# Block products of a feed-forward layer: weights fetched a group ahead, a matmul divided at another column, feature sums reloaded in wider pieces

## The chip, the cores and the metric

The kernel runs on one core of one Trainium2 chip. The metric is the device time of one execution in microseconds (us), the median over the runs. The engines are called as in the profile: PE (TensorE matmul), PEld (TensorE weight load), DVE (VectorE), ACT (ScalarE), POOL (GpSimd), SP (SyncE, which here only issues DMAs).

## What is computed

A block of a diffusion model on 512 tokens and 2048 features: a token mixer (a state-space branch and a long-convolution branch), then a gated feed-forward layer. The change lies in the feed-forward layer alone:

```python
def swiglu(h, wg, wu, wd):
    return (jax.nn.silu(h @ wg) * (h @ wu)) @ wd

h = modulate(x, norm_ffn_pre[layer], sh2, sc2)
x = x + g2 * rmsnorm(swiglu(h, w_gate[layer], w_up[layer], w_down[layer]), norm_ffn_post[layer])
```

`h` has 512 tokens x 2048 features, the two first weights are 2048 x 5632, the last is 5632 x 2048.

## The kernel before

All work is in fp32, done as three matmuls on a number split in two: `hi` is the value rounded to the fp32r type by ACT (a CAST), `lo` is the rest, by DVE (a TENSOR_TENSOR, subtract). A product is then hi·hi + hi·lo + lo·hi. Tiles of split weights are `whi` and `wlo` (three buffers each), those of split features `fh`/`fl` and `th`/`tl`.

Most of the feed-forward layer is a loop over 54 **quads** (`quad(q)`). A quad is a 2x2 group of weight blocks, each 128x1024, times a 2x2 group of feature blocks, computed with seven block products instead of eight (a Strassen-like scheme). The quads come as gate, up, gate, up, ... for 38 of them, 0 to 37 (even ones of `w_gate`, odd ones of `w_up`), then 16 of `w_down` (`w_ds`), 38 to 53.

Each of the seven products is a `body`, 8 x 3 matmuls of 256 columns, so a quad has 168 matmuls. `body` 0 to 6 use the weights r11, r12, r22, r21, r11 again, r22 again, r12 again. Between them the weights are changed in place: r21 gets the fourth block added and r11 the third block, both by an accumulating DMA that POOL issues (L163, `accum_op=ADD`); then DVE adds r11 into r22 and r22 into r12 (L80, `rq<-rq,rq`). `feed` does for each body: ACT cast to `whi`, DVE subtract to `wlo`, and then gives the matmuls of the body fed two steps before. So a body's weights are split two bodies ahead of their matmuls. A call of `feed` is a **step**, seven to a quad.

After the products DVE forms the four results R of the quad (`early` after body 5, `end` after body 6). In an up quad `end` multiplies with the gate's R, SP stores R to `hd` (L163, `hd<-R`), DVE forms sums T of R that the seven products of `w_down` need (`sums`, three operations), and SP stores T (`hd<-T`). The last pairs, blocks 19 to 21, have no T. In the gate quads a piece of an unrelated vector product is carried along (`ada`: a load `rt<-in_ada` into the buffer that T also uses, then two DVE operations `ada<-rt,cc,ada`).

At quad 38 and again at quad 46 the features are exchanged (`replace`): the products' eight input tiles are loaded from `hd` in 128x256 pieces and split by ACT and DVE (L1368, L1370), six sets of eight pieces spread over the steps, two splits of a set in a step.

Order: the loop's loads and splits stay in program order on their queues (`keep_in_program_order`), SP issues its DMAs one after the other, and a DMA that has to wait (for a buffer, or for the result that it stores) holds all that stand behind it. The other operations on DVE and ACT are placed by a scheduler.

The first matmul of body 0 is divided in two, columns 0 to 159 and 160 to 255, in every third quad (`KICK = 160`, `q % 3 == 0`).

Of the kernel before, what the change touches and what calls it, by code (L numbers as in the profile page):

```python
# [65 lines left out]
def block_kernel(ctx: ExitStack, tc: tile.TileContext, I: dict, out: bass.AP, dbg=None, stop=None):  # L66
    nc = tc.nc
# [11 lines left out]
    def tt(e, o, a, b, op):  # L79
        e.tensor_tensor(out=o, in0=a, in1=b, op=op)  # L80
# [87 lines left out]
    def wraw(ap):  # L168
        raw = wp.tile([128, 1024], F32, tag="raw", bufs=3, name=nm("raw"))
        n = ap.shape[-1]  # L170
        dma(raw[:, :n], ap)
        return raw

    def wload(ap, eng=nc.vector):
        raw = wraw(ap)
        n = ap.shape[-1]
        hi = wp.tile([128, 1024], F32R, tag="whi", bufs=3, name=nm("whi"))
        lo = wp.tile([128, 1024], F32R, tag="wlo", bufs=3, name=nm("wlo"))
        nc.scalar.copy(out=hi[:, :n], in_=raw[:, :n])  # L179
        tt(eng, lo[:, :n], raw[:, :n], hi[:, :n].bitcast(F32), SUB)  # L180
        return [(hi[:, o : min(o + 128, n)], lo[:, o : min(o + 128, n)]) for o in range(0, n, 128)]
# [1140 lines left out]

    CH = ([3 + i for i in range(8)], [11 + i for i in range(8)])
    CP = [0, 1, 2, 19, 20, 21]
    KICK = 160

    def place(j, k, area):
        if j == 0:
# [12 lines left out]
    def at(n, fn):  # L1341
        hooks.setdefault(n, []).append(fn)
# [20 lines left out]
    def op_load(dst, src):  # L1363
        dma(dst[1].bitcast(F32), src)
# [6 lines left out]

    def replace(q, c, area):

        for j in range(1, 7):
            n = 7 * (q - 1) + j
            for k in range(8):
                d = place(j, k, 0)
                at(n + 3, lambda d=d, k=k, j=j: op_load(d, hd[CH[c][k]][:, SRC[j], :]))
                at(n + 5 + k // 2, lambda d=d: op_split(d))
        for k in range(8):  # L1380
            d = place(0, k, area)
            at(7 * (q - 4) + k, lambda d=d, k=k: op_load(d, hd[CH[c][k]][:, 0, :]))
            at(7 * (q - 4) + k + 2, lambda d=d: op_split(d))
# [9 lines left out]
        dma(raw, ap)  # L1393
        return raw

    def load_s1(q):
        r = qload("raw", quads[q][0][1, 0])
        dma(r, quads[q][0][1, 1], nc.gpsimd, accum_op=ADD)
        return r

    y2d = dram.tile([2, 8, 128, 4, 256], F32, name="y2d")
    gate = {}
    pin[0] = True
# [4 lines left out]
        return raw  # L1408

    ada_raw[0] = raw_t  # L1410
    nxt = {"r11": qload("ra", quads[0][0][0, 0]), "r12": qload("ra", quads[0][0][0, 1]), "r21": load_s1(0)}

    def quad(q):
        src, area, kind, m = quads[q]
        ps = {}
        R = gu.tile([128, 4, 256], F32, tag="R", bufs=2, name=nm("R"))

        def body(i):
            def run(w):
                if i in (0, 2, 3, 5):  # L1420
                    ps[i] = acc()
                b, o = {0: (0, 0), 1: (0, 1), 2: (2, 1), 3: (3, 1), 4: (3, 0), 5: (5, 0), 6: (2, 0)}[i]
                p = ps[b][:, o * 256 : o * 256 + 256]
                for k in range(8):
                    xh, xl = place(i, k, area)
                    wh, wl = w[k]

                    for c0, c1 in ((0, KICK), (KICK, 256)) if i == k == 0 and q % 3 == 0 else ((0, 256),):
                        nc.tensor.matmul(p[:, c0:c1], wh, xh[:, c0:c1], start=k == 0 and c0 == 0, stop=False,  # L1429
                                         skip_group_check=True)  # L1430
                    nc.tensor.matmul(p, wh, xl, start=False, stop=False, skip_group_check=True)  # L1431
                    nc.tensor.matmul(p, wl, xh, start=False, stop=k == 7, skip_group_check=True)  # L1432
                if i == 5:
                    late.append(early)
                if i == 6:
                    late.append(end)

            return run

        def early():  # L1440
            p12, p75, p6 = ps[0], ps[3], ps[5]
            nc.scalar.copy(out=R[:, 0, :], in_=p12[:, 0:256])
            tt(nc.vector, R[:, 0, :], p6[:, 0:256], R[:, 0, :], SUB)
            tt(nc.vector, R[:, 2, :], R[:, 0, :], p75[:, 0:256], SUB)
            tt(nc.vector, R[:, 1:4:2, :], R[:, 0:4:2, :], p75[:, 256:512].unsqueeze(1).broadcast_to([128, 2, 256]), ADD)
            nc.scalar.copy(out=R[:, 0, :], in_=p12[:, 0:256])
            tt(nc.vector, R[:, 0, :], R[:, 0, :], p12[:, 256:512], ADD)

        def end():

            tt(nc.vector, R[:, 1:3, :], R[:, 1:3, :], ps[2].rearrange("p (a b) -> p a b", a=2), SUB)
            if kind == "w_gate":
                act(R[:, 0, :], R[:, 0, :], AF.Silu)
                act(R[:, 1, :], R[:, 1, :], AF.Silu, scale=-1.0)
                act(R[:, 2:4, :], R[:, 2:4, :], AF.Silu)
# [12 lines left out]

        def sums(m, R):
            T = gu.tile([128, 4, 256], F32, tag="T", name=nm("T"))  # L1470
            tt(nc.vector, T[:, 0:4:2, :], R[:, 1:4:2, :], R[:, 0:2, :], SUB)
            tt(nc.vector, T[:, 1, :], R[:, 3, :], T[:, 0, :], SUB)
            tt(nc.vector, T[:, 3, :], T[:, 1, :], R[:, 2, :], SUB)
            dma(hd[m][:, 4:8, :], T)


        r11, r12, r21 = nxt["r11"], nxt["r12"], nxt["r21"]
        more = q + 1 < len(quads)
        r22 = qload("raw", src[1, 1])
        feed(r11, body(0))  # L1480
        feed(r12, body(1))
        feed(r22, body(2))
        dma(r11, src[1, 0], nc.gpsimd, accum_op=ADD)
        feed(r21, body(3))
        if more:
            nxt["r11"] = qload("ra", quads[q + 1][0][0, 0])
        feed(r11, body(4))
        if more:
            nxt["r21"] = load_s1(q + 1)
        tt(nc.vector, r22, r22, r11, ADD)  # L1490
        feed(r22, body(5))
        if more:
            nxt["r12"] = qload("ra", quads[q + 1][0][0, 1])
        tt(nc.vector, r12, r12, r22, ADD)
        feed(r12, body(6))
        if kind != "w_up" and q < NG + 4:
            ada(1)

# [16 lines left out]
        quad(q)  # L1515
    while pend:
        pend.pop()()
    first = [wload(I["w_dc"][0])]

    def rest():  # L1520
        for op in late:
# [6 lines left out]
    rest()  # L1528
    w, fn = ahead.pop(0)
    fn(w)  # L1530
    first.append(wload(I["w_dc"][1]))
    rest()
    w, fn = ahead.pop(0)
    fn(w)
# [227 lines left out]
```

## Time and profile before

| | us |
|---|---|
| median of 3 runs | 2620.09 (2610.10 to 2623.55) |
| profiled execution | 2608.34 |
| its span, first to last instruction | 2606.6 |
| quads 0 to 37 (gate, up) | 809.76 |
| quads 38 to 53 (w_down) | 340.1 |
| all 54 quads, of the span | 1149.85 |

Quads 0 to 53 run from 1278.03 to 2427.88 us of the span, and what lies ahead of and behind them is not touched by the change, except for the two first loads behind the last quad. A quad's start is the start of the first matmul of its body 0. PE is busy for 2410.9 of 2606.6 us, but matmuls overlap, so what a quad costs is read from its length, not from the busy time. DVE is busy for 1880.5 us, ACT for 985.4 us.

### The profile page before, as it was taken

The numbers are of one execution on the slowest core, as the hardware profiler recorded it, in microseconds if no ns is written. First come the engines' busy times: TensorE is split into PE (matmuls) and PEld (weight loads), VectorE is DVE, ScalarE is ACT, GpSimd is POOL, SyncE is SP. The second block draws the span as 40 slices with busy tenths as digits, with TensorE's granted clock in tenths as the row PEclk, the third lists the DMA queues.
The fourth block names the chain that finished last, engine by engine and source line by source line (L and its number), as shares of the span: only waits on it lengthen the run. The fifth ranks groups of instructions, "written<-read, shape, count | busy, mean of one in ns | idle before, by whom it ended". The sixth has DMA issues, their size and how long they took to land.

```text
span 2606.6 us, 41025 instructions
## 1 busy us (share of the span) xinstructions
PE 2410.9 (92%) x16102; PEld 2145.6 (82%) x16102; DVE 1880.5 (72%) x2494; ACT 985.4 (38%) x1437; POOL 554.7 (21%) x537
## 2 busy tenths in 40 slices
PE   8999989899999999999998999999989989899895
PEld 3467779577667788989998999899989989899785
DVE  7986756888878776789776767676767776677444
ACT  3143325222123322455434343343434444444233
POOL 1230010665623245740000000000000000000104
PEclk9999999999999999999999999999999999999998
DMA  8867745445356666456857575757576777877843
GB/s 289 319 214 244 228 156 165 146 139 171 114 197 201 242 230 205 149 175 188 236 146 211 160 212 158 209 159 208 157 210 171 209 229 217 227 213 182 261 135 121
DMA packets 183721, 508.71 MB, mean 195 GB/s; under 512 B 19583, under 2 KB 65599, under 8 KB 181992
## 3 DMA queue, kind: packets, MB, share of 16 engines
q1 hardware_dynamic: 166824, 445.27, 50.3%
q0 software_dynamic: 16704, 60.82, 13.2%
q8 instruction: 126, 2.06, 0.3%
q14 instruction: 67, 0.55, 0.1%
HBM read 454.12 MB, written 51.90 MB: 194 GB/s over the span
## 4 chain that ended last, share of the span: by engine, by line
PE 34%; DMA 13%; DVE 5%; issue 3%; ACT 2%; POOL 1%; SPq 0%; POOLq 0%; DVEq 0%; ACTq 0%
DMA rq<-in_w_up 9%; PE acc L1432 9%; PE acc L1431 9%; PE acc L1429 9%; PE acc L83 8%; DVE wlo L80 2%; DMA rq<-in_w_ds 1%; ACT whi L1347 1%; DMA x<-x1d 1%; DMA y<-y2d 1%; DMA rt<-in_ada 0%; DVE R L80 0%; DMA tl<-hd 0%; POOL gs L80 0%; POOL rq L163 0%
## 5 line engine op out<-in xcount | busy, mean ns | idle before, releaser
L1347 ACT CAST whi<-rq 128x1024 fp32r<-128x1024 f32 x378 | 397.3, 1051 | 614.5 <-PE acc L1431 376.2
L80 DVE TENSOR_TENSOR wlo<-rq,whi 128x1024 fp32r<-128x1024 f32 x378 | 459.3, 1222 | 187.6 <-ACT whi L1347 183.2
L1432 PE MATMUL acc<-th,wlo 128*128 128x256 f32 x1728 | 491.7, 285 | 50.6 <-DVE wlo L80 50.6
L1429 PE MATMUL acc<-th,whi 128*128 128x256 f32 x1728 | 489.4, 283 | 10.5 <-ACT whi L1347 10.5
L1431 PE MATMUL acc<-tl,whi 128*128 128x256 f32 x1728 | 488.8, 283 | 0.0
L179 ACT CAST whi<-raw 128x1024 fp32r<-128x1024 f32 (+1 forms) x220 | 225.7, 1026 | 503.5 <-PE acc L83 295.5
L1432 PEld LDWEIGHTS acc<-th,wlo 128*128 128x128 f32 x1728 | 334.6, 194 | 55.3 <-DVE wlo L80 55.2
L1429 PE MATMUL acc<-fh,whi 128*128 128x256 f32 (+2 forms) x1314 | 362.2, 278 | 4.4 <-ACT fh L1368 4.4
L1432 PE MATMUL acc<-fh,wlo 128*128 128x256 f32 x1296 | 361.7, 279 | 2.5 <-DVE wlo L80 2.5
L1431 PE MATMUL acc<-fl,whi 128*128 128x256 f32 x1296 | 362.2, 279 | 0.0
L80 DVE TENSOR_TENSOR wlo<-raw,whi 128x1024 fp32r<-128x1024 f32 x204 | 265.4, 1301 | 121.2 <-ACT whi L179 116.4
L1429 PEld LDWEIGHTS acc<-th,whi 128*128 128x128 f32 x1728 | 334.8, 194 | 11.4 <-ACT whi L1347 11.4
L1431 PEld LDWEIGHTS acc<-tl,whi 128*128 128x128 f32 x1728 | 335.6, 194 | 0.0
L83 PE MATMUL acc<-hh,whi 128*128 128x512 f32 x688 | 285.1, 416 | 3.9 <-ACT hh L74 3.7
L83 PE MATMUL acc<-hl,whi 128*128 128x512 f32 x688 | 277.6, 403 | 3.6 <-DVE hl L77 3.6
L83 PE MATMUL acc<-hh,wlo 128*128 128x512 f32 x688 | 276.9, 402 | 0.0
L1429 PEld LDWEIGHTS acc<-fh,whi 128*128 128x128 f32 x1314 | 247.0, 189 | 4.8 <-ACT fh L1368 4.5
L1432 PEld LDWEIGHTS acc<-fh,wlo 128*128 128x128 f32 x1296 | 244.8, 189 | 3.4 <-DVE wlo L80 3.3
L1431 PEld LDWEIGHTS acc<-fl,whi 128*128 128x128 f32 x1296 | 245.8, 190 | 0.1
L77 DVE SCALAR_TENSOR_TENSOR ada<-raw,cc,ada 128x512 f32<-128x512 f32 x200 | 171.7, 859 | 45.2 <-DMA raw<-in_ada 42.3
L80 DVE TENSOR_TENSOR rq<-rq,rq 128x1024 f32<-128x1024 f32 x108 | 131.9, 1221 | 97.4 <-DMA rq<-in_w_up 85.6
L83 PE MATMUL acc<-fh,wlo 128*128 128x256 f32 (+1 forms) x512 | 160.0, 313 | 14.4 <-DVE wlo L80 14.4
(333 smaller groups left out, 4513.6 us busy)
## 6 DMA issues: line engine op xcount, KB each, us to landing
raw<-in_ada SPq DMA_DIRECT2D x107, 512.0 KB, 4.1
rq<-in_w_gate SPq DMA_DIRECT2D x76, 512.0 KB, 9.6
rq<-in_w_up SPq DMA_DIRECT2D x76, 512.0 KB, 5.8
ada<-in_ada SPq DMA_DIRECT2D x64, 512.0 KB, 4.4
rq<-in_w_ds SPq DMA_DIRECT2D x64, 512.0 KB, 5.7
raw<-in_w_hy SPq DMA_DIRECT2D x44, 512.0 KB, 4.0
raw<-in_w_out SPq DMA_DIRECT2D x41, 512.0 KB, 4.2
raw<-in_w_xbc SPq DMA_DIRECT2D x38, 512.0 KB, 4.0
```

The source lines that it names most:

```text
L77: nc.vector.scalar_tensor_tensor(out=o, in0=a, scalar=s, in1=b, op0=op0, op1=op1)
L80: e.tensor_tensor(out=o, in0=a, in1=b, op=op)
L83: nc.tensor.matmul(o, lhsT, rhs, start=start, stop=stop)
L179: nc.scalar.copy(out=hi[:, :n], in_=raw[:, :n])
L1347: nc.scalar.copy(out=hi, in_=raw)
L1429: nc.tensor.matmul(p[:, c0:c1], wh, xh[:, c0:c1], start=k == 0 and c0 == 0, stop=False, skip_group_check=True)
L1431: nc.tensor.matmul(p, wh, xl, start=False, stop=False, skip_group_check=True)
L1432: nc.tensor.matmul(p, wl, xh, start=False, stop=k == 7, skip_group_check=True)
```

## The change

1. **Weights.** Each quad issues the loads of all four weight blocks of the next quad: r11 ahead of its first `feed`, r12 and r21 after it, r22 after the fifth. Before, r11, r21 and r12 of the next quad were issued after the fourth, fifth and sixth `feed`, and r22 of the quad itself at its start. The accumulating DMA into r11 is issued after the second `feed` (before: the third), and the one into r21 of the next quad right behind it. Buffers are as many as before. Behind the last quad the two first blocks of the next stage come the same way.
2. **Division of a matmul.** At 16 columns (16 and 240) in place of 160 (160 and 96), in every second quad in place of every third, that is in 27 quads in place of 18.
3. **Feature sums.** At quads 38 and 46, four of the six sets are loaded in pairs, 128x512 a piece, and split in pieces of that size, four in a step. The two others stay as they were.

```diff
-    def wload(ap, eng=nc.vector):
-        raw = wraw(ap)
+    def wload(ap, eng=nc.vector, raw=None):
+        raw = wraw(ap) if raw is None else raw
...
-    KICK = 160
+    KICK = 16
...
     def replace(q, c, area):
-        for j in range(1, 7):
-            n = 7 * (q - 1) + j
+        n = 7 * (q - 1)
+        for j, load, first in ((1, 4, 6), (6, 9, 11)):
             for k in range(8):
                 d = place(j, k, 0)
-                at(n + 3, lambda d=d, k=k, j=j: op_load(d, hd[CH[c][k]][:, SRC[j], :]))
-                at(n + 5 + k // 2, lambda d=d: op_split(d))
+                at(n + load, lambda d=d, k=k, j=j: op_load(d, hd[CH[c][k]][:, SRC[j], :]))
+                at(n + first + k // 2, lambda d=d: op_split(d))
+        for o, load, first in ((2, 7, 9), (0, 8, 10)):
+            for k in range(8):
+                d = [t[:, o : o + 2, :] for t in tx[k]]
+                at(n + load, lambda d=d, k=k, o=o: op_load(d, hd[CH[c][k]][:, 4 + o : 6 + o, :]))
+                at(n + first + k // 4, lambda d=d: op_split(d))
...
-                    for c0, c1 in ((0, KICK), (KICK, 256)) if i == k == 0 and q % 3 == 0 else ((0, 256),):
+                    for c0, c1 in ((0, KICK), (KICK, 256)) if i == k == 0 and q % 2 == 0 else ((0, 256),):
...
-        r11, r12, r21 = nxt["r11"], nxt["r12"], nxt["r21"]
+        r11, r12, r21, r22 = nxt
         more = q + 1 < len(quads)
-        r22 = qload("raw", src[1, 1])
+        nsrc = quads[q + 1][0] if more else None
+        n11 = qload("ra", nsrc[0, 0]) if more else None
         feed(r11, body(0))
+        n12 = qload("ra", nsrc[0, 1]) if more else None
+        n21 = qload("raw", nsrc[1, 0] if more else I["w_dc"][0])
         feed(r12, body(1))
+        dma(r11, src[1, 0], nc.gpsimd, accum_op=ADD)
+        if more:
+            dma(n21, nsrc[1, 1], nc.gpsimd, accum_op=ADD)
         feed(r22, body(2))
-        dma(r11, src[1, 0], nc.gpsimd, accum_op=ADD)
         feed(r21, body(3))
-        if more:
-            nxt["r11"] = qload("ra", quads[q + 1][0][0, 0])
         feed(r11, body(4))
-        if more:
-            nxt["r21"] = load_s1(q + 1)
         tt(nc.vector, r22, r22, r11, ADD)
+        n22 = qload("raw", nsrc[1, 1] if more else I["w_dc"][1])
         feed(r22, body(5))
-        if more:
-            nxt["r12"] = qload("ra", quads[q + 1][0][0, 1])
         tt(nc.vector, r12, r12, r22, ADD)
         feed(r12, body(6))
```

Three places show what moves. The first is SP's queue in a gate quad, here quad 4, up to the loads of the up quad behind it; of that up quad, quad 5, rq_11877, 11908, 11941 and 11977 are r11, r21, r12 and r22 before.

```order
L163 DMA hd<-R_11519 128x1024
L163 DMA hd<-T_11818 128x1024
L163 DMA rq_11877<-in_w_up 128x1024
L163 DMA rq_11908<-in_w_up 128x1024
L163 DMA rq_11941<-in_w_up 128x1024
L163 DMA rt_11972<-in_ada 128x1024
L163 DMA rq_11977<-in_w_up 128x1024
```

The same place in the changed kernel, where r11, r12, r21 and r22 of quad 5 are rq_11746, 11777, 11779 and 11915.

```order
L163 DMA rq_11746<-in_w_up 128x1024
L163 DMA rq_11777<-in_w_up 128x1024
L163 DMA rq_11779<-in_w_up 128x1024
L163 DMA hd<-R_11522 128x1024
L163 DMA hd<-T_11826 128x1024
L163 DMA rq_11915<-in_w_up 128x1024
L163 DMA rt_11975<-in_ada 128x1024
```

Three of the four loads of the up quad now stand ahead of the two stores, and `rt` has one load ahead of it instead of three.

The second place is DVE from the end of the gate quad to the subtraction for body 3 of the up quad (the same quad 5). Before:

```order
L80 TENSOR_TENSOR wlo_11980<-rq_11877,whi_11979 128x1024
L80 TENSOR_TENSOR R_11743<-acc_11983,R_11743 128x256
L80 TENSOR_TENSOR R_11743<-R_11743,acc_11916 128x256
L77 SCALAR_TENSOR_TENSOR ada_7630<-rt_11972,cc,ada_7630 128x512
L80 TENSOR_TENSOR R_11743<-R_11743,acc_11916 128x2x256
L77 SCALAR_TENSOR_TENSOR ada_7630<-rt_11972,cc,ada_7630 128x512
L80 TENSOR_TENSOR R_11743<-R_11743,acc_11823 128x256
L80 TENSOR_TENSOR wlo_12009<-rq_11941,whi_12008 128x1024
L80 TENSOR_TENSOR R_11743<-R_11743,acc_11883 128x512
L80 TENSOR_TENSOR wlo_12043<-rq_11977,whi_12042 128x1024
L80 TENSOR_TENSOR rq_11977<-rq_11977,rq_11877 128x1024
L80 TENSOR_TENSOR wlo_12077<-rq_11908,whi_12076 128x1024
```

And in the changed kernel, from `ada` on:

```order
L77 SCALAR_TENSOR_TENSOR ada_7630<-rt_11975,cc,ada_7630 128x512
L80 TENSOR_TENSOR wlo_11983<-rq_11746,whi_11982 128x1024
L77 SCALAR_TENSOR_TENSOR ada_7630<-rt_11975,cc,ada_7630 128x512
L80 TENSOR_TENSOR R_11745<-acc_11986,R_11745 128x256
L80 TENSOR_TENSOR R_11745<-R_11745,acc_11921 128x256
L80 TENSOR_TENSOR wlo_12016<-rq_11777,whi_12015 128x1024
L80 TENSOR_TENSOR R_11745<-R_11745,acc_11921 128x2x256
L80 TENSOR_TENSOR R_11745<-R_11745,acc_11889 128x512
L80 TENSOR_TENSOR wlo_12052<-rq_11915,whi_12051 128x1024
L80 TENSOR_TENSOR R_11745<-R_11745,acc_11831 128x256
L80 TENSOR_TENSOR rq_11915<-rq_11915,rq_11746 128x1024
L80 TENSOR_TENSOR rq_11777<-rq_11777,rq_11915 128x1024
```

The subtraction for body 3 (`wlo_12085<-rq_11779,whi_12084`) is the next row. Two things moved: the first `ada` operation now stands ahead of the subtraction of r11 for body 0, and both additions, not one, stand ahead of the subtraction of r21 for body 3.

The third place is SP around quad 38, where the features are exchanged. Before, r22 of quad 38 is rq_19563, behind three sets of eight `tl` pieces, the last pieces being these:

```order
L163 DMA tl_10294<-hd 128x256
L163 DMA tl_10354<-hd 128x256
L163 DMA tl_10412<-hd 128x256
L163 DMA tl_10472<-hd 128x256
L163 DMA rq_19563<-in_w_ds 128x1024
L163 DMA tl_10082<-hd 128x256
```

In the changed kernel r22 of quad 38 is rq_19490, behind the eight `fl` pieces of the first set and ahead of all `tl` pieces; rq_19555 is r11 of quad 39:

```order
L163 DMA fl_9088<-hd 128x256
L163 DMA fl_9094<-hd 128x256
L163 DMA fl_9100<-hd 128x256
L163 DMA rq_19490<-in_w_ds 128x1024
L163 DMA rq_19555<-in_w_ds 128x1024
L163 DMA tl_10082<-hd 128x512
```

r22 no longer waits behind the pieces, and loads of quad 39 now stand among them.

## Rows read from the trace of the kernel before

**Rows 1.** Windows, single quads: length, busy us (count) by engine, PEclk, DMA share, GB/s
```profile
1278.03:2087.79 809.76, 760.74 (x6415) 756.65 (x6414) 564.15 (x684) 327.63 (x412) 67.03 (x76) 0.97 0.66 187
1360.13:1379.17 19.04, 19.04 (x171) 19.04 (x170) 14.75 (x21) 7.91 (x9) 1.77 (x2) 1.00 0.69 234
1379.17:1402.01 22.84, 19.30 (x170) 19.11 (x169) 15.01 (x17) 9.15 (x12) 1.75 (x2) 1.00 0.62 153
2028.33:2048.11 19.78, 19.78 (x170) 19.78 (x169) 14.79 (x19) 9.75 (x14) 2.05 (x3) 1.00 0.56 124
2048.11:2068.00 19.89, 19.89 (x171) 19.89 (x170) 15.82 (x20) 7.89 (x9) 1.77 (x2) 1.00 0.82 240
2184.20:2203.36 19.16, 19.16 (x171) 19.16 (x170) 15.12 (x21) 10.14 (x16) 1.78 (x2) 1.00 0.86 231
2313.53:2332.68 19.15, 19.15 (x171) 19.15 (x170) 13.40 (x15) 8.22 (x10) 1.75 (x2) 1.00 0.74 193
```

**Rows 2.** Waits of PE, quads 0 to 37: us in total, times, longest
```profile
PE acc L1432 <- DVE wlo L80: 48.0, 17, 4.5
```

**Rows 3.** Timeline of SP, quad 4: start, us, what it issues
```profile
1368.76 0.33 SPq L163 DMA_DIRECT2D hd<-T  x1
1369.19 1.67 SPq L163 DMA_DIRECT2D rq<-in_w_up  x3
1372.23 0.33 SPq L163 DMA_DIRECT2D rt<-in_ada  x1
```

**Rows 4.** Timeline of POOL, quads 3 to 5, accumulating DMAs
```profile
1357.49 0.87 POOL L163 DMA_DIRECT2D rq<-in_w_gate  x1 [14.73 <-DVE wlo L80]
...
1376.46 1.83 POOL L163 DMA_DIRECT2D rq<-in_w_up  x2 [18.10 <-DMA rq<-in_w_up]
```

**Rows 5.** Timeline of DVE, quad 5 (up)
```profile
1378.36 0.75 DVE L77 SCALAR_TENSOR_TENSOR ada<-rt,cc,ada 128x512 f32<-128x512 f32 x1 [0.58 <-DMA rt<-in_ada]
1379.03 0.68 DVE L80 TENSOR_TENSOR R<-R,acc 128x512 f32<-128x512 f32 x1
...
1380.29 0.41 DVE L80 TENSOR_TENSOR R<-R,acc 128x256 f32<-128x256 f32 x1
...
1382.35 1.22 DVE L80 TENSOR_TENSOR wlo<-rq,whi 128x1024 fp32r<-128x1024 f32 x1
1388.84 1.23 DVE L80 TENSOR_TENSOR rq<-rq,rq 128x1024 f32<-128x1024 f32 x1 [5.27 <-DMA rq<-in_w_up]
1389.98 1.22 DVE L80 TENSOR_TENSOR wlo<-rq,whi 128x1024 fp32r<-128x1024 f32 x1
```

**Rows 6.** DMAs, median us to landing: quads 0-33; quad 35's r11; `rt`'s range
```profile
rq<-in_w_up POOLq DMA_DIRECT2D x34, 512.0 KB, 9.8
rq<-in_w_gate POOLq DMA_DIRECT2D x34, 512.0 KB, 5.6
...
hd<-T SPq DMA_DIRECT2D x16, 512.0 KB, 3.4
...
rq<-in_w_up POOLq DMA_DIRECT2D x1, 512.0 KB, 6.7
...
DMA to landing us min/median/max: 4.9/6.3/8.3
```

**Rows 7.** Quads 38, 46, part of 38 (windows); SP and ACT in 38 (timelines)
```profile
2087.79:2120.38 32.59, 24.83 (x170) 23.12 (x168) 29.51 (x62) 21.22 (x53) 0.87 (x1) 0.84 0.88 274
2260.60:2294.49 33.89, 22.60 (x170) 21.49 (x169) 26.40 (x55) 21.93 (x53) 1.14 (x2) 0.90 0.89 262
2097.40:2118.86 21.46, 18.03 (x115) 16.85 (x116) 21.44 (x46) 16.98 (x42) 0.87 (x1) 0.79 0.86 275
...
2089.51 0.33 SPq L163 DMA_DIRECT2D rq<-in_w_ds  x1
2089.94 10.17 SPq L163 DMA_DIRECT2D tl<-hd  x16
...
2096.04 1.04 ACT L1347 CAST whi<-rq 128x1024 fp32r<-128x1024 f32 x1 [3.07 <-DMA rq<-in_w_ds]
```

More of the change, by code (lines that the diff above doesn't have):

```diff
@@ L1394, in qload @@
         return raw
[L1396 to L1399, printed above, removed]
     y2d = dram.tile([2, 8, 128, 4, 256], F32, name="y2d")
@@ L1410, in block_kernel @@
     ada_raw[0] = raw_t
-    nxt = {"r11": qload("ra", quads[0][0][0, 0]), "r12": qload("ra", quads[0][0][0, 1]), "r21": load_s1(0)}
+    nxt = [qload(t, quads[0][0][i, j]) for t, i, j in (("ra", 0, 0), ("ra", 0, 1), ("raw", 1, 0), ("raw", 1, 1))]
+    dma(nxt[2], quads[0][0][1, 1], nc.gpsimd, accum_op=ADD)
     def quad(q):
@@ L1474, in sums @@
             dma(hd[m][:, 4:8, :], T)
-        r11, r12, r21 = nxt["r11"], nxt["r12"], nxt["r21"]
+        r11, r12, r21, r22 = nxt
         more = q + 1 < len(quads)
-        r22 = qload("raw", src[1, 1])
+        nsrc = quads[q + 1][0] if more else None
+        n11 = qload("ra", nsrc[0, 0]) if more else None
         feed(r11, body(0))
+        n12 = qload("ra", nsrc[0, 1]) if more else None
+        n21 = qload("raw", nsrc[1, 0] if more else I["w_dc"][0])
         feed(r12, body(1))
+        dma(r11, src[1, 0], nc.gpsimd, accum_op=ADD)
+        if more:
+            dma(n21, nsrc[1, 1], nc.gpsimd, accum_op=ADD)
         feed(r22, body(2))
-        dma(r11, src[1, 0], nc.gpsimd, accum_op=ADD)
         feed(r21, body(3))
-        if more:
-            nxt["r11"] = qload("ra", quads[q + 1][0][0, 0])
         feed(r11, body(4))
-        if more:
-            nxt["r21"] = load_s1(q + 1)
         tt(nc.vector, r22, r22, r11, ADD)
+        n22 = qload("raw", nsrc[1, 1] if more else I["w_dc"][1])
         feed(r22, body(5))
-        if more:
-            nxt["r12"] = qload("ra", quads[q + 1][0][0, 1])
         tt(nc.vector, r12, r12, r22, ADD)
         feed(r12, body(6))
+        nxt[:] = [n11, n12, n21, n22]
         if kind != "w_up" and q < NG + 4:
@@ L1517, in block_kernel @@
         pend.pop()()
-    first = [wload(I["w_dc"][0])]
+    first = [wload(I["w_dc"][0], raw=nxt[2])]
     def rest():
@@ L1530, in block_kernel @@
     fn(w)
-    first.append(wload(I["w_dc"][1]))
+    first.append(wload(I["w_dc"][1], raw=nxt[3]))
     rest()
```

## The prediction

> **What bounds the kernel now.** I read the lengths of single quads first, because PE's busy time counts overlapping matmuls. A gate quad without trouble takes 19.04 us for 168 matmuls, 113 ns each, at the full clock; the up quad behind it takes 22.84 us [rows 1]. 38 quads of 19.04 us would be 723.5 us, and quads 0 to 37 take 809.76: 86.3 us too many. Three things make these up. PE waits for DVE's subtraction `wlo` 17 times, 48.0 us in all [rows 2]. The mean granted clock is 0.97 [rows 1], and the clock has two levels here, 2.4 and 1.2 GHz, so about (1 - 0.97) / 0.5 x 809.76 = 49 us ran at 1.2 GHz, of which half, 24 us, is lost. The other 14 us are a second rhythm: quad 35 has the full clock and no wait and still takes 19.78 us, 118 ns a matmul [rows 1]. That is 0.74 us a quad.
>
> Then I read one pair, quads 4 and 5, and count from the start of gate quad 4 (1360.13). SP issues the T store at +8.6 (1368.76); only then come three loads for the up quad, and POOL can issue the two accumulating DMAs of the up quad only when these have landed, both together at 1376.46 [rows 3, 4]. They take 9.8 us at the median there, against 5.6 us in gate quads, where r11's goes out alone 2.6 us ahead of the quad's start [rows 4, 6]. DVE stands 5.27 us before its addition into r22, which waits for the second of them; the subtraction for body 3 stands right behind it [rows 5]. So the chain is: T store, loads, accumulation, addition, subtraction, PE. PE waits at the first lo·hi matmul of body 3, in the up quads, and the clock often falls after it. Quad 35, an up quad ahead of which no T is stored, has no such wait [rows 1]. That is the best sign that the chain is rightly read.
>
> The exchanges have other limits. Quads 38 and 46 take 32.59 and 33.89 us. In 38, r22's load stands behind pieces of features in SP's queue and is issued 1.7 us after the quad has begun, ACT waits 3.07 us for it, and from 2097.40 to 2118.86 DVE is busy for 21.44 of 21.46 us [rows 7].
>
> **The change part by part.**
>
> Weights ahead. In the changed order r11, r12 and r21 of the up quad stand ahead of the T store, so their loads land before the up quad needs them; r21's accumulation runs during the gate quad. That removes the cause of the present wait. What is late next is r11's accumulation in the up quad, which must wait until DVE has subtracted r11 for body 0, and that subtraction now stands behind the first `ada`, which waits for `rt`. `rt` still waits for the T store to land, since it uses T's buffer: it was issued at 1372.23, +12.1, 3.5 us after the store, about the store's median of 3.4 [rows 3, 6]. The new chain, with durations from DVE's rows [rows 5]:
> - `rt` lands at L = 12.1 + 4.9 = 17.0. Its landing takes 4.9 to 8.3 us [rows 6]; in quad 4 the `ada` shows it at 18.2. I take the low end, because one load stands ahead of it instead of three.
> - `ada` 0.75 and the subtraction 1.22 bring L + 2.0, when POOL issues the accumulation.
> - It lands A later. Bounds are 5.6 (alone) and 9.8 (two together, with loads beside); quad 35's, alone with loads beside, took 6.7 [rows 6]. I take 6.0, nearest to the lone ones.
> - Behind it come two additions and the subtraction for body 3, 3 x 1.22 less some overlap, 3.5 us with their waits. The weights of body 3 are then ready at L + A + 5.5. DVE's own work between (second `ada`, two `R` of 0.41, two of 0.68, two subtractions, one more `R`) ends at about L + 7.4, slightly ahead of the landing.
> - PE wants them at 19.04 + 3 x 2.72 + 0.23 = 27.4.
>
> The wait per up quad is therefore L + A - 21.9 = 1.1 us, with bounds 0.7 (17.0 and 5.6) and 6.1 (18.2 and 9.8). It does not add up from quad to quad, as the chain begins anew with each gate quad's T. With such short waits I leave 5 of the 24 us to the clock.
>
> The gate quads' chain is unchanged: r11's accumulation goes out at -2.6 and has until about 8 us later before body 3 is late (the addition ran at +3.8, the subtraction ended 1.6 us ahead of need). The earlier loads may stand beside it: cost 0, and up to 1 us in a gate quad if it took 9.8.
>
> A rule of the Trainium skill speaks against this part. Accumulations beside loads take 9.8 us and alone 5.6 [rows 6]; the skill's page "DMA: Bandwidth & Descriptors", section "Issuing engines are not separate DMA queues", says that DMAs run on the same 16 engines and interleave, whichever engine began them. Loads fetched earlier are then more traffic beside r11's accumulation, and the third rival would be the outcome.
>
> Division of a matmul. A divided one adds 0.11 us to a quad (19.15 against 19.04, [rows 1]); nine more quads have one, 1 us. Whether 16 columns do more than 160 no row shows. At 160 one of them ended the slow rhythm (quad 42: 19.16, with the quad ahead at 19.79) and one did not (quad 36: 19.89) [rows 1]. With fewer waits to disturb PE and more divided matmuls I leave 7 of the 12 us that the slow rhythm costs; the bounds are 0 and 38 x 0.74 = 28.
>
> Exchanges. r22's load no longer stands behind pieces, so the idle time of DVE can go. It is 32.59 - 29.51 = 3.1 us in quad 38 and 33.89 - 26.40 = 7.5 in quad 46 [rows 7]. Wider splits take 0.68 for what took 2 x 0.41, 16 of them in each exchange: 2 us at the most. DVE then remains the bound, at some 28 us. Against it, three loads of the next quad now stand among the pieces. I take 4 us off quad 38, 6 off quad 46, and 2 off quad 39, which starts late now: 12 in all, with bounds of -11 (below) and +20.
>
> Behind the last quad the two loads come earlier; PE does not wait there for them, so nothing is gained.
>
> **The sum.** Quads 0 to 37: 723.5 + 19 x 1.1 + 5 (clock) + 7 (rhythm) + 19 x 0.11 = 758.5, or 51 us less. The exchanges give 12. Together 63: the profiled execution's 2608.3 would become 2545. The median before lies 12 us above that execution, for which no row gives a reason; I add 5 of them and predict 2550.
>
> **The rivals.**
>
> 1. No wait is left and PE stays in the quick rhythm: 723.5 + 2.1, 84 us less, and 18 from the exchanges: 2506, with the 5 us 2511. For it: quad 35 runs without a wait. Against it: its `rt` did not wait for a T.
> 2. The division at 16 columns does not end the slow rhythm, or starts it. All 54 quads at 19.78 cost 40 us where my sum has some 9: 31 more, 2581. For it: quad 36 stayed slow. Against it: that was at 160.
> 3. Slower than before: the accumulation meets the loads that were fetched early. With 18.2 and 9.8 the wait is 6.1 us per up quad, 116 in all; with clock and rhythm as now (24 + 13) and 2 for the divisions, quads 0 to 37 take 879, 69 more, and the exchanges give 12 back: 2665, with the 5 us 2670. It decides from L + A = 25.0 on, a wait of 3.1 us, where 19 waits eat all that is won. For it: the two bounds are medians of today. Against it: loads for the up quad will have landed long before, and r21's accumulation too.
> 4. The exchanges get worse: 1.5 MB of next weights ahead of the last pieces, at 274 GB/s [rows 7], are 5.7 us for each exchange, and the 12 us are not won: 23 more, 2573.
> 5. Waits of about 2.5 to 3.5 us in the up quads: no change to speak of, 2600 to 2625.
>
> **How the numbers follow.** The forecast (2530 to 2570) has a chance of 0.47, rival 1 0.15, rival 2 0.14, rival 4 0.10, rival 5 0.06, rival 3 0.08. I leave out rivals 3 and 5 and the outer part of rival 1: 2512 to 2590. A measurement of this kernel can tell some 0.5%, 13 us, from no change. Faster by more than that are the forecast and rivals 1, 2 and 4, with a remainder for an exchange and a rhythm that go wrong together: 0.86. Within it: 0.06. Slower: 0.08.
>
> **What would show it.** In the profile after, the store of T should have no load of the next up quad's r11, r12 or r21 behind it; POOL should issue the up quad's two accumulations far apart, r11's at about +19 of the pair, landing in about 6 us. DVE's longest wait in the up quad should be at `ada` for `rt` (ended near +17), not at the addition. PE's waits for `wlo` in quads 0 to 37 should come to some 20 us with few stretches at 1.2 GHz, gate quads should stay at 19.04, and quad 38 should take about 28.5. I am wrong in the main if the up quads still wait for 3 us or more, at body 3 or at body 0; in the second term if quads of 19.8 us without a wait are the rule; in the third if quads 38 and 46 take longer than now.

## The result, and the profile after

The changed kernel takes 2542.91 us (median of 4 runs, 2542.11 to 2548.92) against 2619.39 us before (4 runs, 2610.10 to 2623.55): a ratio of 0.9718, 95% interval 0.9688 to 0.9748. A second set of runs gave 2541.36 us and 0.9713 (0.9684 to 0.9741). The profiled execution took 2548.92 us, its span 2547.1. The medians are 76.5 us apart, the two profiled executions only 59.4: the one before is faster than each of its four runs, the one after is the slowest of its four.

Windows of the profile after, columns as in [rows 1]: quads 0 to 37; quads 4 and 5; quad 21 (up); quads 38 and 46; quads 38 to 53.

```profile
1278.30:2030.60 752.30, 746.17 (x6421) 744.16 (x6420) 569.26 (x685) 327.16 (x410) 66.98 (x76) 1.00 0.73 202
1358.88:1378.04 19.16, 19.16 (x172) 19.16 (x171) 15.35 (x22) 7.91 (x9) 1.28 (x2) 1.00 0.76 237
1378.04:1397.63 19.59, 19.32 (x171) 19.13 (x169) 14.51 (x16) 9.26 (x12) 2.02 (x3) 1.00 0.70 171
1695.64:1715.45 19.81, 19.81 (x170) 19.81 (x169) 13.73 (x16) 9.14 (x12) 1.77 (x2) 1.00 0.67 165
2030.60:2063.19 32.59, 25.82 (x171) 24.30 (x170) 28.60 (x47) 19.95 (x37) 1.76 (x2) 0.79 0.79 257
2206.55:2238.19 31.64, 24.44 (x171) 22.53 (x170) 26.00 (x42) 20.41 (x38) 1.78 (x2) 0.84 0.80 258
2030.60:2371.84 341.24, 325.26 (x2707) 321.64 (x2706) 250.86 (x307) 162.24 (x233) 26.49 (x30) 0.96 0.72 207
```

Nearly all of what the two profiles differ by lies in quads 0 to 37: 809.76 us became 752.30. Quads 38 to 53 took 340.1 and take 341.24; quad 38 has not moved (32.59 both times). The waits of PE in quads 0 to 37, as in [rows 2], fell from 48.0 us for `wlo` to 3.0:

```profile
PE acc L1433 <- DVE wlo L80: 3.0, 3, 2.4
PE aux L83 <- DVE ada L77: 2.0, 2, 1.4
PE acc L1430 <- DVE R L80: 1.0, 3, 0.4
```

SP and POOL in quad 4, which now starts at 1358.88 (timelines; compare [rows 3, 4]):

```profile
1367.51 0.33 SPq L163 DMA_DIRECT2D hd<-T  x1
1367.96 0.35 SPq L163 DMA_DIRECT2D rq<-in_w_up  x1
1370.87 0.33 SPq L163 DMA_DIRECT2D rt<-in_ada  x1
...
1358.39 0.88 POOL L163 DMA_DIRECT2D rq<-in_w_up  x1 [1.28 <-DMA rq<-in_w_up]
1376.90 0.89 POOL L163 DMA_DIRECT2D rq<-in_w_up  x1 [17.64 <-DVE wlo L80]
```

Behind the store of T stands one load, r22's; the two accumulations of the up quad go out 18.5 us apart, r21's at -0.5 and r11's at +18.0 of the pair. DVE around the start of quad 5 (timeline; compare [rows 5]):

```profile
1374.61 0.75 DVE L77 SCALAR_TENSOR_TENSOR ada<-rt,cc,ada 128x512 f32<-128x512 f32 x1 [2.30 <-DMA rt<-in_ada]
1375.28 1.22 DVE L80 TENSOR_TENSOR wlo<-rq,whi 128x1024 fp32r<-128x1024 f32 x1
...
1383.17 2.49 DVE L80 TENSOR_TENSOR rq<-rq,rq 128x1024 f32<-128x1024 f32 x2 [1.23 <-DMA rq<-in_w_up]
1385.58 3.49 DVE L80 TENSOR_TENSOR wlo<-rq,whi 128x1024 fp32r<-128x1024 f32 x3
```

The long wait (5.27 us before) stands at `ada` now, for `rt`, and is 2.30 us. Landings, median us, quads 0 to 33 (compare [rows 6]):

```profile
rq<-in_w_up POOLq DMA_DIRECT2D x33, 512.0 KB, 5.7
rq<-in_w_gate POOLq DMA_DIRECT2D x32, 512.0 KB, 5.5
rt<-in_ada SPq DMA_DIRECT2D x17, 512.0 KB, 3.6
...
hd<-T SPq DMA_DIRECT2D x16, 512.0 KB, 3.0
```

The accumulations of the up quads fell from 9.8 to 5.7 us. Each of these medians is taken over two kinds, r21's and r11's. Counted apart (the up quads 3 to 33), r21's took 9.0 us before and r11's, issued right behind it, 11.6; r11's now takes 5.4. In the exchanges a new wait has come (SP, ACT of quad 38, timelines; then the longest wait of ACT and PE's in quad 46):

```profile
2038.74 8.01 SPq L163 DMA_DIRECT2D fl<-hd  x8
...
2046.84 0.71 ACT L1368 CAST fh<-fl 128x256 fp32r<-128x256 f32 x2 [5.01 <-DMA fl<-hd]
2047.46 2.17 ACT L1368 CAST th<-tl 128x512 fp32r<-128x512 f32 x4
...
ACT fh L1368 <- DMA fl<-hd: 4.9, 1, 4.9
...
2224.70 0.58 PE L1430 MATMUL acc<-th,whi 128*128 128x256 f32 x1 [5.18 <-ACT th L1368]
```

ACT waits for the first of the last eight `fl` pieces, which only body 6 needs, and four `th` casts stand behind it. Each of these writes the halves for body 3 and for body 5, and PE stops at the first of the two: counted from the quad's start, this matmul is that of the fifth weight block of body 3. In quad 38 PE stops at the same matmul, for less long (a gap of 1.9 us), after a gap of 2.9 us for `wlo` at the start of body 3. The clock falls with it: by the granted clock, quads 38 and 46 ran 13.7 and 10.2 us at 1.2 GHz, before 10.2 and 6.8.

### The profile page after: what moved, and what is told of

The parts are those of the page before. It is cut to its first block, busy times and chain, and to the rows that moved or that the text cites. A ratio compares the mean times of both kernels' runs of the same rounds, so it can differ in the third digit from the quotient of the medians.

```text
span 2547.1 us, 40917 instructions
## 1 busy us (share of the span) xinstructions
PE 2404.7 (94%) x16111; PEld 2139.3 (84%) x16111; DVE 1883.5 (74%) x2462; ACT 981.9 (39%) x1405; POOL 556.0 (22%) x537
## 4 chain that ended last, share of the span: by engine, by line
PE 39%; DMA 7%; DVE 7%; issue 2%; ACT 1%; POOL 1%; SPq 0%; POOLq 0%; DVEq 0%; ACTq 0%
PE acc L1430 11%; PE acc L1433 11%; PE acc L1432 11%; PE acc L83 5%; DVE wlo L80 3%; DMA rt<-in_ada 1%; DMA hd<-T 1%; DMA tl<-hd 1%; DMA rq<-in_w_up 1%; DMA fl<-hd 1%; DVE y L80 1%; DMA rq<-in_w_gate 1%; DVE R L80 1%; DMA y<-y2d 1%; DMA x<-x1d 0%
## 5 line engine op out<-in xcount | busy, mean ns | idle before, releaser
L1433 PE MATMUL acc<-th,wlo 128*128 128x256 f32 x1728 | 486.3, 281 | 7.3 <-DVE wlo L80 7.2
L1430 PE MATMUL acc<-fh,whi 128*128 128x256 f32 (+1 forms) x1323 | 364.5, 278 | 1.0 <-DVE R L80 1.0
L1433 PEld LDWEIGHTS acc<-th,wlo 128*128 128x128 f32 x1728 | 329.3, 191 | 8.8 <-DVE wlo L80 8.7
L1432 PEld LDWEIGHTS acc<-tl,whi 128*128 128x128 f32 x1728 | 329.7, 191 | 4.2 <-DVE tl L1370 4.1
L83 PEld LDWEIGHTS acc<-hh,whi 128*128 128x128 f32 x688 | 133.4, 194 | 39.9 <-ACT hh L74 6.0
```

The source lines that it names most:

```text
L83: nc.tensor.matmul(o, lhsT, rhs, start=start, stop=stop)
```

## The experiments

All kernels compute the whole output. Times are medians in us; the ratio is to the kernel before in the same set of runs; the last two columns are from the profiled execution.

| kernel | median | ratio (95% interval) | quads 0-37 | 38-53 |
|---|---|---|---|---|
| before | 2619.4 | | 809.8 | 340.1 |
| changed | 2542.9 | 0.9718 (0.9688-0.9748) | 752.3 | 341.2 |
| changed, once more | 2541.4 | 0.9713 (0.9684-0.9741) | 752.0 | 338.6 |
| 1 weights alone | 2545.7 | 0.9730 (0.9697-0.9763) | 747.4 | 337.8 |
| 2 store of T later | 2580.1 | 0.9865 (0.9831-0.9899) | 779.1 | 339.9 |
| 3 accumulations together | 2614.7 | 0.9977 (0.9956-0.9999) | 796.0 | 344.3 |
| 4 division as before | 2538.4 | 0.9703 (0.9666-0.9741) | 746.4 | 337.5 |
| 5 no division | 2550.9 | 0.9742 (0.9715-0.9768) | 757.6 | 335.8 |
| 6 division in every quad | 2542.6 | 0.9714 (0.9692-0.9737) | 741.0 | 335.6 |
| 7 `ada` in the up quads | 2532.5 | 0.9676 (0.9650-0.9703) | 730.2 | 339.9 |
| 8 last pieces later | 2538.5 | 0.9691 (0.9663-0.9719) | 744.9 | 333.2 |
| 9 both, 7 and 8 | 2522.2 | 0.9634 (0.9609-0.9659) | 734.4 | 329.4 |
| 10 and no `ada` in 38 | 2516.2 | 0.9610 (0.9587-0.9633) | 734.4 | 326.9 |
| 11 and body 2 earlier | 2520.5 | 0.9631 (0.9608-0.9654) | 733.9 | 328.6 |

**1. Weights alone.** The changed kernel with the division and `replace` of before:

```diff
-    KICK = 16
+    KICK = 160
...
-        n = 7 * (q - 1)
-        for j, load, first in ((1, 4, 6), (6, 9, 11)):
+        for j in range(1, 7):
+            n = 7 * (q - 1) + j
...
-for c0, c1 in ((0, KICK), (KICK, 256)) if i == k == 0 and q % 2 == 0 else ((0, 256),):
+for c0, c1 in ((0, KICK), (KICK, 256)) if i == k == 0 and q % 3 == 0 else ((0, 256),):
```

> Before with the first part alone: loads a quad ahead, r21's accumulation in the quad ahead; the division stays at 160 columns in every third quad, and the pieces stay 256 wide. My theory (the gain is the up quads' wait, whose head was the store of T ahead of the loads): PE's waits for wlo in quads 0 to 37 fall from 48 us to under 10, quads 0 to 37 take 750 to 765 us, the median is within 8 us of the changed kernel: 2535 to 2555. Rival (a good part came from the division at 16 columns): quads 0 to 37 take 770 us or more, median 2560 to 2590. Rival (the wide pieces gave some of it): quads 38 to 53 longer than 350 us.

Waits of PE in quads 0 to 37 of this kernel:

```profile
PE acc L1428 <- DVE wlo L80: 2.9, 4, 1.3
PE aux L83 <- DVE ada L77: 2.1, 2, 1.4
```

2545.72 us and 747.4 for quads 0 to 37: the first part alone gives all the gain that can be measured. Quads 38 to 53 are no longer than with wide pieces (337.8 against 341.2 and 338.6), so the wide pieces gave nothing that shows.

**2. The store of T later.** Before, with one store moved; it now stands behind three of the next quad's four loads, and r22's behind it, as before:

```diff
-            dma(hd[m][:, 4:8, :], T)
+            tstore.append((m, T))
...
             nxt["r12"] = qload("ra", quads[q + 1][0][0, 1])
+        while tstore:
+            mt, Tt = tstore.pop()
+            dma(hd[mt][:, 4:8, :], Tt)
```

> Before with one thing moved: SP issues the store of T behind the four loads of the next quad instead of ahead of three of them. All else, the order of the loads and both accumulations too, stays. My theory (the store of T, which waits for DVE's sums, holds the loads): the loads for an up quad go out some 4 us earlier, its two accumulations no longer go out together, PE's waits for wlo in quads 0 to 37 fall from 48 us to under 15, and the time to 2550 to 2580 (rt comes about 2 us later than before, so some waits move to ada). Rival (the loads are late for another reason, or the accumulations are slow whenever they start): waits of 35 us or more stay, 2605 to 2625.

Waits of PE in quads 0 to 37; SP and POOL in quad 4 (it starts at 1359.71); landing of the two accumulations, in order, and the plain DMAs' traffic (packets, MB, share of 16 engines) during the second:

```profile
PE acc L1429 <- DVE R L80: 13.7, 11, 2.2
PE acc L1432 <- DVE wlo L80: 9.4, 8, 2.0
PE aux L83 <- DVE ada L77: 6.5, 2, 3.8
...
1364.09 1.67 SPq L163 DMA_DIRECT2D rq<-in_w_up  x3
1368.35 0.33 SPq L163 DMA_DIRECT2D hd<-T  x1
...
1370.69 0.88 POOL L163 DMA_DIRECT2D rq<-in_w_up  x1 [12.74 <-DMA rq<-in_w_up]
1376.15 0.89 POOL L163 DMA_DIRECT2D rq<-in_w_up  x1 [4.59 <-DVE wlo L80]
...
rq<-in_w_up POOLq DMA_DIRECT2D x1, 512.0 KB, 5.7
...
rq<-in_w_up POOLq DMA_DIRECT2D x1, 512.0 KB, 8.8
...
q1 hardware_dynamic: 659, 2.43, 73.1%
```

The loads go out at +4.4 in place of +9.1, and the waits for `wlo` fall from 48.0 to 9.4 us: the store of T was the head of the chain. 2580.05 us stands on the edge of what was expected, as two other things are left. r11's accumulation, issued 5.5 us behind r21's now, still takes 8.8 us (9.5 at the median of the up quads 3 to 33): `rt`, r22 and three loads for the next gate quad were issued in the 2.6 us before it, and plain DMAs hold 73% of the engines (15% beside the 6.2 us of the same accumulation in the changed kernel). And `rt` comes later, so `ada` holds DVE's operations on R, for which PE waits 13.7 us.

**3. Accumulations together.** The changed kernel with r21's accumulation back in its own quad:

```diff
         dma(r11, src[1, 0], nc.gpsimd, accum_op=ADD)
-        if more:
-            dma(n21, nsrc[1, 1], nc.gpsimd, accum_op=ADD)
+        dma(r21, src[1, 1], nc.gpsimd, accum_op=ADD)
```

> The changed kernel with one thing taken back: r21's accumulation is issued in its own quad, right behind r11's, as far as the loads that it needs have long landed. If two accumulations together are slow by themselves (the 9.8 us of the median of before), r21's lands about 18 + 0.9 + 9.8 = +28.7 in an up quad, where body 3 wants it by about +24, and by about the same too late in a gate quad: 4 to 5 us for each of most quads, 2640 to 2700, slower than before. Rival (they were slow because of the loads that landed beside them; each takes about 6 us here): at most about 1 us a quad, 2545 to 2575.

Landing of r11's and r21's accumulation of quad 5, the plain DMAs' traffic meanwhile, and ACT's cast of r21 there:

```profile
rq<-in_w_up POOLq DMA_DIRECT2D x1, 512.0 KB, 5.4
...
rq<-in_w_up POOLq DMA_DIRECT2D x1, 512.0 KB, 8.5
...
q1 hardware_dynamic: 131, 0.44, 11.9%
...
1392.64 1.99 ACT L1347 CAST whi<-rq 128x1024 fp32r<-128x1024 f32 x2 [3.70 <-DMA rq<-in_w_up]
```

2614.68 us: neither number was met. The first of the two takes what a lone one takes, the second 8.5, with hardly any plain DMA beside them (11.9%). At the median of the up quads 3 to 33 it is 5.5 and 7.7, so being together costs the second 2 to 3 us. That is enough, as r21 lands at +28 where its cast for body 3 should begin near +25 (an estimate: 27.4, when PE wants the weights, less a cast of 1.05 and a subtraction of 1.22). Quads 0 to 37 lose 44 us in the profile (which is the fastest of this kernel's runs; the medians are 72 us apart). So loads issued early are not worth much while r21's accumulation goes out behind r11's in its own quad: having it in the quad ahead is what makes the first part work.

**4 to 6. The division.** The changed kernel with 160 columns in every third quad; with none; and at 16 columns in every quad (beside the changed kernel once more):

```diff
-    KICK = 16
+    KICK = 160
...
-for c0, c1 in ((0, KICK), (KICK, 256)) if i == k == 0 and q % 2 == 0 else ((0, 256),):
+for c0, c1 in ((0, KICK), (KICK, 256)) if i == k == 0 and q % 3 == 0 else ((0, 256),):
```

```diff
-for c0, c1 in ((0, KICK), (KICK, 256)) if i == k == 0 and q % 2 == 0 else ((0, 256),):
+for c0, c1 in ((0, 256),):
```

```diff
-for c0, c1 in ((0, KICK), (KICK, 256)) if i == k == 0 and q % 2 == 0 else ((0, 256),):
+for c0, c1 in ((0, KICK), (KICK, 256)) if i == k == 0 else ((0, 256),):
```

> The changed kernel with the old division, 160 and 96 columns in every third quad. My theory (a division ends the 118 ns rhythm about one time in four at either size, 2 of 7 at 160, 4 of 15 at 16): within 8 us of the changed kernel, 2535 to 2555; quads at 19.8 us make 10 to 20 us in all. Rival (16 columns, or twice as many divided matmuls, keep the rhythm quick): the quads of 19.8 us become the rule, 20 to 28 us in all, 2555 to 2570.

> The changed kernel with no matmul divided. My theory (a division ends the 118 ns rhythm one time in four, and costs 0.11 us): once begun, the slow rhythm lasts until the next longer stall; of quads 0 to 37 more than 25 take 19.8 us, quads 0 to 37 take 755 to 766 us, the median 2545 to 2556. Rival (the division does nothing that stalls don't do too): within 4 us of the changed kernel or a little below it, 2536 to 2546.

> The changed kernel itself, beside the next ones. All theories: 2540 to 2550; it gives the middle by which the kernels without a division and with one in every quad are read.

> The changed kernel with the first matmul divided at 16 in every quad, 54 in place of 27. My theory (each division that meets the 118 ns rhythm ends it about one time in three and never begins it): the quads of 19.8 us in 0 to 37 fall from 16 to about 8 to 12, which gives 3 to 6 us, and the added divisions cost 27 x 0.11 = 3 us: 2536 to 2546, no difference to speak of from the changed kernel. Rival (a division is what decides the rhythm): under 2534.

The medians are 2538.43, 2550.93 and 2542.61 against 2542.91 and 2541.36 of the changed kernel. Column and number of the divisions make no difference that can be measured. Without any it is some 9 us slower, but the intervals overlap (0.9715 to 0.9768 against 0.9684 to 0.9741): likely, not shown. Single profiles vary: of quads 0 to 37, 17 take 19.8 to 19.9 us where none is divided (more than 25 were expected), 16 and 13 in the changed kernel, 8 with the old division, 3 with one in every quad. Experiment 1 has the old division too, and 17 such quads.

**7. `ada` in the up quads.** What is left of the waits has one place. Quad 12 to 13 of the changed kernel, DVE and PE (timelines):

```profile
1534.16 0.75 DVE L77 SCALAR_TENSOR_TENSOR ada<-rt,cc,ada 128x512 f32<-128x512 f32 x1 [3.24 <-DMA rt<-in_ada]
...
1536.63 0.41 DVE L80 TENSOR_TENSOR R<-acc,R 128x256 f32<-128x256 f32 x1
...
1536.53 0.28 PE L1433 MATMUL acc<-fh,wlo 128*128 128x256 f32 x1
1537.19 0.36 PE L1430 MATMUL acc<-fh,whi 128*128 128x256 f32 x1 [0.39 <-DVE R L80]
```

DVE waits 3.24 us for `rt`; the operation on R that frees PE's accumulator stands behind, and PE starts body 0 of quad 13 half a microsecond late. From quad 13 to 15 the quads take 19.62, 19.90 and 19.79 us. The experiment moves the call:

```diff
         feed(r21, body(3))
+        if kind != "w_gate" and q < NG + 4:
+            ada(1)
...
-        if kind != "w_up" and q < NG + 4:
-            ada(1)
```

> The changed kernel with the ada piece carried in the up quads, behind the fourth step, instead of at the end of the gate quads: the same loads and operations in the same number, but rt then finds T's buffer free. My theory (what is left of the waits in quads 0 to 37 comes from rt standing behind the store of T: ada waits for it, and behind ada stand the subtraction of r11 and the operations on R that free PE's accumulators; such a wait of some 0.5 us also begins the 118 ns rhythm): DVE waits nowhere for rt, the gaps at the start of up quads and ahead of body 3 go, PE's waits in quads 0 to 37 fall from 6.0 to 3 us or less (quad 0 keeps its 2.4), quads 0 to 37 take 732 to 745 us instead of 752.3, the median 2525 to 2537. Rival (the rhythm comes by itself, and the waits were too small to matter): 748 to 754 us, 2538 to 2548.

Quads 0 to 37 (window), and the only row of PE's waits in them:

```profile
1280.47:2010.70 730.23, 728.99 (x6422) 728.79 (x6420) 568.72 (x685) 325.73 (x410) 66.86 (x76) 1.00 0.76 208
...
PE acc L1433 <- DVE wlo L80: 1.2, 1, 1.2
```

DVE's waits for `rt` in these quads, of the changed kernel and of this one:

```profile
DVE ada L77 <- DMA rt<-in_ada: 32.1, 16, 3.2
...
DVE ada L77 <- DMA rt<-in_ada: 7.1, 9, 1.3
```

DVE still waits for `rt`, against the expectation, but for less long, and PE no longer waits behind it. 35 of 38 quads take 19.04 or 19.2 us. The rows of PE's waits show 6.0 us in the changed kernel, and 22 are gone between the two profiles: the rest is the slow rhythm, and in two quads the 1.2 GHz, that followed them. The medians show 10 of the 22 (2532.48 against 2542.91), as single profiles vary. What holds over all of them: in the four kernels with `ada` moved (7, 9, 10, 11) quads 0 to 37 take 730 to 734 us, with 0 to 2 quads at 19.8; in the seven that keep the changed order and do not move it (changed twice, 1, 4, 5, 6, 8) they take 741 to 758, with 3 to 17. Had the rhythm come by itself, as the rival has it, the two groups would not lie apart.

**8. Last pieces later.** The changed kernel with the last set's splits moved:

```diff
-        for j, load, first in ((1, 4, 6), (6, 9, 11)):
+        for j, load, first, per in ((1, 4, 6, 2), (6, 9, 13, 4)):
...
-                at(n + first + k // 2, lambda d=d: op_split(d))
+                at(n + first + k // per, lambda d=d: op_split(d))
```

> The changed kernel with one thing moved in the exchanges: the last set of eight fl pieces is split two steps later, four in a step, so that ACT doesn't stand waiting for these pieces (5.0 us in quad 38, 4.9 in 46) with the cast of tl pieces that PE needs sooner behind it. My theory (that wait took the place of the one for r22, which is why quads 38 and 46 hardly gained): quad 38 falls from 32.6 to 26 to 29 us, quad 46 from 31.65 to 25 to 29, the median by 6 to 11 us to 2531 to 2537. Rival (DVE's own work or the landing of the pieces bounds the exchange): both quads stay within 1.5 us, 2539 to 2548.

Quad 46 and quad 38 (windows), and DVE in quad 38 (timeline):

```profile
2199.48:2226.33 26.85, 24.40 (x172) 22.04 (x171) 25.75 (x42) 20.39 (x38) 2.25 (x3) 0.94 0.94 308
2026.75:2059.16 32.41, 24.61 (x172) 23.38 (x170) 28.69 (x47) 20.09 (x37) 1.75 (x2) 0.86 0.87 273
...
2050.35 0.75 DVE L77 SCALAR_TENSOR_TENSOR ada<-rt,cc,ada 128x512 f32<-128x512 f32 x1 [2.82 <-DMA rt<-in_ada]
```

Quad 46 falls from 31.64 to 26.85 us. Quad 38 stays: there the next wait is for `rt`, which SP issues behind the `fl` pieces. The median, 2538.48, is 3 to 4 us lower, less than the 6 to 11 expected and not clear of the noise.

**9 to 11.** Both moves; then quad 38's `ada` carried in quad 42; then also the pieces of body 2 loaded two steps earlier, 256 wide (the second diff):

```diff
-        if kind != "w_gate" and q < NG + 4:
+        if kind != "w_gate" and q != NG and q < NG + 5:
```

```diff
-        for j, load, first, per in ((1, 4, 6, 2), (6, 9, 13, 4)):
+        for j, load, first, per in ((1, 4, 6, 2), (2, 5, 7, 2), (4, 7, 9, 2), (6, 9, 13, 4)):
-        for o, load, first in ((2, 7, 9), (0, 8, 10)):
+        for o, load, first in ((0, 8, 10),):
```

> The changed kernel with both moves, ada in the up quads and the last fl pieces split two steps later. If the two are independent, as my theory has it, the gains add: 2514 to 2532. Rival (each stall ended frees work that collides elsewhere, or neither is a cause): 2535 or more.

> The kernel with both moves (ada in the up quads, last fl pieces split later), and quad 38's ada carried in quad 42 instead. There DVE waited 3.8 us for rt, which stood behind the fl pieces on SP, with the subtraction for body 4 and the addition into r12 behind the ada. My theory: quad 38 falls from 33.4 to 27 to 30 us, the median to 2513 to 2520. Rival (the landing of pieces or r11's accumulation is late at the same place): quad 38 stays within 1.5 us, 2519 to 2525.

> As the kernel without quad 38's ada, and in the exchanges the pair of sets of which body 2 needs one half is taken apart again: body 2's pieces are loaded two steps earlier, 256 wide, and split in the quad ahead, where DVE has room. My theory (DVE bounds the first half of quad 38): 8 splits of 0.41 us leave it, quads 38 and 46 fall by 2 to 3.5 us each, the median to 2507 to 2515. Rival (SP's issues and the landing of the pieces bound it; 256-wide splits cost 0.41 for half of 0.68): within 2 us of it, 2512 to 2521.

Quads 38 and 46 of kernel 10 (windows), a run of wide splits in its quad 38, and one of narrow ones in quad 38 of kernel 11 (DVE timelines):

```profile
2013.59:2040.32 26.73, 22.30 (x172) 21.52 (x170) 26.54 (x44) 19.97 (x37) 1.76 (x2) 0.94 1.00 324
2179.03:2204.56 25.53, 22.80 (x172) 20.46 (x170) 25.27 (x41) 20.12 (x38) 1.78 (x2) 1.00 1.01 321
...
2021.19 4.90 DVE L1370 TENSOR_TENSOR tl<-tl,th 128x512 fp32r<-128x512 f32 x8
...
2022.47 2.77 DVE L1370 TENSOR_TENSOR tl<-tl,th 128x256 fp32r<-128x256 f32 x8
```

The two moves add up as expected (2522.22). Without quad 38's `ada`, quad 38 falls from 33.36 to 26.73 us, and DVE is busy for 26.54 of them: now DVE is the bound, which it was not yet in the changed kernel (28.60 of 32.59). Part of what is won against that kernel's 32.59 us is the clock: 3.4 us at 1.2 GHz in place of 13.7 (PEclk 0.94 and 0.79), worth 5 us at most. 2516.21 us is the best of all, 25 us below the changed kernel in the same set. Kernel 11 gained nothing more (2520.49, quads 27.10 and 26.43): six of body 2's eight splits still ran in quad 38. Its narrow splits take 0.35 us each in a row, the wide ones 0.61, so width saves 0.08 us on two.

## Why the prediction was right, and where it was wrong

2550 was predicted, 2542.91 came, inside the range. Against the profiled execution the sum was 2545, and that execution took 2548.92. The terms did worse than the sum: in quads 0 to 37 the change gave 57.5 us where 51 were predicted, in the exchanges (quads 38, 39 and 46) 2 where 12 were, and nothing of it is left in quads 38 to 53 (340.1 before, 341.24 after). That these errors, with 3 us of the tail, cancel to 4 us is luck.

- **The reading of before: three sizes off.** The 0.97 of the clock is a rounded row: by the granted clock 41.0 us ran at 1.2 GHz, not 49, so 20 are lost, not 24. The gaps between matmuls come to 53 us, more than the 48.0 of the `wlo` row. With 3 us for matmuls of `ada` that PE does in two of the quads (quads 9 and 25 of kernel 7 take 20.47 us by them, in place of 19.04), and 1 for the divisions, that leaves some 9 for the slow rhythm, not 14. And 9.8 us for "both together" is the median of r21's 9.0 and r11's 11.6, so the upper bound of the wait, 6.1, should have been near 8 (18.2 and 11.6).
- **The cause of the old wait: right, and incomplete.** Experiment 2 shows the store of T as the head of the chain. But the prediction took the 9.8 us as something that goes with two accumulations at once and with loads beside them, and did not part the two. Experiments 2 and 3 do, for r11's or the second one, at the median of the up quads 3 to 33: 9.5 behind loads, 7.7 as the second of two with few loads beside them, 5.4 in the changed kernel, 11.6 before with both. The change removes both.
- **The new chain: right in its steps, 1 us too long.** `ada` for `rt` is the late one, as named. L was put at 17.0 and is 15.5 (median, 14.7 to 16.7), since `rt` lands in 3.6 us at the median, less than the least row of before, 4.9; r11's accumulation goes out at +17.8 instead of about +19, A is 5.4 instead of 6.0, and it lands at +23.5. L + A = 20.9 lies below the 21.9 of the formula: no wait. Where both were late, in quad 5 (15.7 and 6.2), the formula gives 0.0 and the trace 0.4. So 19 x 1.1 = 21 us came out as three short stalls at body 3, of 0.4 us at most (quads 5, 33 and 35); with the others (quad 0, `aux` and R behind `ada`) the stalls come to some 8.
- **Rhythm: the mis-sized term of this part.** 7 us were left for it. 752.3 less 723.5, 2 for the divisions, 8 of stalls, 3.4 for the clock (6.8 us at 1.2 GHz; 5 were predicted) and 3 for the matmuls of `ada` leaves 12, more than the 9 of before. I priced a short wait at its length. Experiment 7 shows the real price. Waits 13 too high, rhythm 5 and `ada`'s matmuls 3 too low: these offset each other to 6 us.
- **Division: right.** It costs 0.12 us (19.16 against 19.04), and 16 columns in place of 160 change nothing that the runs can tell. Rival 2 was half there: quads of 19.8 us without a wait are 16 of 38, where before had 7.
- **Exchanges: wrong.** The step that failed is "the idle time of DVE can go": r22 does land in time, but a new wait of 5.0 us, ACT's for the last `fl` pieces, took the place of the 3.07 for r22. I had weighed the loads among the pieces and not the casts that stand behind a piece which isn't there yet. That 12 us lay in the exchanges is shown by kernel 10: 26.73 and 25.53 us, 12 less than the changed kernel in the two quads; but it took two moves that the change doesn't make. DVE as the bound, "at some 28 us", came true only there, at 26.5. Wide splits were put at up to 2 us an exchange; at 0.08 us a pair it is 1.3.
- **The tail: no change, as predicted.** Behind the last quad 175.3 us follow, 178.7 before; in the other profiles it is 175.8 to 181.0.
- **From the profile to the median: wrong sign.** I added 5 us; the median lies 6 below the profiled execution. Quad 0 starts anywhere from 1272.35 to 1284.36 us in the fourteen profiles, in a part that no kernel here changes; so much is left to chance, and the 5 us had no ground.
- **Rivals 3 and 4.** The mechanism of rival 3 is real (9.5 us beside loads, experiment 2), but it did not meet r11's accumulation: L + A is 20.9, and it decides at 25.0. The rule of the Trainium skill that was set against this part ("DMA: Bandwidth & Descriptors", section "Issuing engines are not separate DMA queues": DMAs from all engines interleave on the same 16) agrees with experiment 2. It did not decide here, since the early loads have landed by then (plain DMAs hold 15% of the engines beside r11's accumulation). Rival 4's 12 us that are not won came true, by another mechanism; its 5.7 us on top did not show.

## What to carry to other kernels

Look for the store that waits for arithmetic and stands ahead of loads in an in-order queue, and move the loads, with any accumulation that hangs on them, ahead of it by a whole stage. When a wait is taken away, list what stands behind the *next* late transfer on each engine in order: here a filler (`ada`) and pieces needed last (`fl`) each held work that PE needed first. Waits of half a microsecond are worth removing if they change how the engine runs afterwards.

## What had not been expected of the hardware

PE has two rhythms at the full clock with the same instructions, 113 and 118 ns a matmul of 256 columns, and a stall often changes the one for the other. Worked out from the starts of the quads' matmuls in the fourteen profiles, with the rhythm taken from the 12 matmuls on each side, all at the full clock: of 119 stalls of over 0.3 us that met the quick rhythm, 61 were followed by the slow one; of 51 that met the slow one, 14 were. A division without a stall beside it never began the slow rhythm (0 of 222) and ended it in 30 of 75 cases at 16 columns, in 11 of 23 at 160. What in the engine sets it, no run here shows.

An accumulating DMA of 512 KB landed in 5.4 us at the median (5.2 to 7.0) in the changed kernel's up quads, in 9.5 (8.3 to 10.4) behind loads (experiment 2), in 7.7 (7.4 to 8.7) as the second of two issued 0.6 us apart (experiment 3), and in 11.6 (10.9 to 12.9) as the second of two behind loads (before). The two costs, 4.1 and 2.3 us, come near to adding up. In quad 5, plain DMAs held 15% of the engines beside it in the changed kernel, 73% in experiment 2 and 12% in experiment 3.
